# Banded attention scores: two triangles of a block pair folded into one 128-key square, and unfolded by GpSimd after the transposes

## The chip, the cores and the metric

The kernel runs on one core of a Trainium2 chip. The metric is the device time of one execution in microseconds; the median of a few runs is compared. A profile is one further execution, taken with the hardware profiler. The engines are named as in the profile: PE (TensorE), DVE (VectorE), ACT (ScalarE), POOL (GpSimd), SP (SyncE, which issues transfers).

## The reference

One decoder layer over 2048 tokens of width 1024. A normalised and modulated input `h` goes through one combined projection. Eight heads do forgetting attention over all earlier tokens. Eight query heads in two key/value groups do sliding-window attention with rotary positions and a learned sink; this is the part that the change touches:

```python
kk, vv = with_prev(k), with_prev(v)          # each block of 128 queries sees its own 128 keys and the 128 before
s = jnp.einsum('bnqhgd,bnshd->bnhgqs', qb, kk) * (d ** -0.5)
rel = i + Q_BLOCK - j                         # i: query in the block, j: key among the 256
band = (rel >= 0) & (rel < WINDOW)            # WINDOW = 128
s = jnp.where(mask, s, -jnp.inf)
p = jax.nn.softmax(jnp.concatenate([s, sink], axis=-1), axis=-1)[..., :-1]
out = jnp.einsum('bnhgqs,bnshd->bnqhgd', p, vv)
```

Query i sees, of its own block, the keys 0 to i, and, of the block before, the keys i+1 to 127: two complementary triangles, always 128 keys in all. The first block has no block before it. Each branch's output is gated, both go through one output projection, and the result is normalised and added to the input.

## The kernel before

The program is one sequence of stages: modulation and transposes of the input (to about 148 us), the banded heads together with projections (to about 440 us), the forgetting heads with the remaining projections, and the output projection. Most matrix products are in split f16: each operand is a high and a low half, and three products (high by high, high by low, low by high) replace an f32 one.

The banded heads are done in 32 windows (`Pair(j, i)`: head pair j, query blocks i and i+1; so two heads by two blocks). The order of the work is written out by hand: each engine's queue holds its instructions in the order in which the program records them. The stage's loop does this for window n:

```python
tick()
if n: wd.maxima()
fill(part[0]); tick()
if n: wd.exps()
fill(part[1]); tick(); fill(part[2]); tick(); fill(part[3])
if n: windows[n - 1].pv()
wd.turn()
if n + 1 < NW: windows[n + 1].scores()
```

`fill` puts projection units on PE (three matmuls of 512 columns, line 332, or twelve of 128, line 350) and runs the events that go with them: weight loads, their maximum (`w_max`), its way to DRAM and back to all partitions (`mx_d`, `mxr`, issued by POOL), and the split of weights into halves. `after(k, f)` runs f at the k-th following `tick`, which is how evacuations of PSUM follow the matmuls.

The steps of a window:

- `scores` (line 870): PE writes up to 256 scores for each of 128 queries, two heads and two blocks, into two PSUM banks (`pss`).
- `maxima` (line 883): one fused DVE instruction for each head and block adds the band mask `bmask`, scales, writes the result to `sm_` in SBUF and accumulates the maximum, starting from the sink. POOL copies the sink's value into a 257th column (line 881). `nb` is the negated maximum (line 887).
- `exps` (line 894): ACT takes the exponential of 257 columns, four times, with row sums.
- `turn` (line 903): PE transposes each block of 128 keys in f32, eight for a window, six where the first block of the sequence is in it, into `pxb` (two PSUM banks). At the next tick ACT copies the high half to f16 (line 912), and at the one after that DVE subtracts it for the low half (line 908); both are in `ptb`.
- `pv` (line 922), at the end of the next window: 24 matmuls multiply the transposed probabilities with the values; DVE divides by the sums at the next tick (line 928).

The pools of `pss`, `sm_`, `pxb` and `ptb` have one buffer each. POOL's queue in this stage holds also the stores of the gates (`z_d`, line 374) and of the outputs (`o_d`), and the weight loads.

Of the kernel before, what the change touches and what calls it, by code (L numbers as in the profile page):

```python
# [10 lines left out]
F32 = mybir.dt.float32  # L11
F16 = mybir.dt.float16
BF16 = mybir.dt.bfloat16
I32 = mybir.dt.int32
AF = mybir.ActivationFunctionType
ALU = mybir.AluOpType
AX = mybir.AxisListType

P = 128
# [7 lines left out]
EPS = 1e-6  # L27
PS_SCALE = 2.0 ** -25
NEG = -1.0e30
VB = P + 8  # L30
LIFT = 10.0 * math.log(2.0)
LIFT_A = 3.0 * math.log(2.0)
# [9 lines left out]
def hybrid_layer(  # L42
# [17 lines left out]
    V, A, G, PE, SP = nc.vector, nc.scalar, nc.gpsimd, nc.tensor, nc.sync  # L60
# [12 lines left out]
    const = ctx.enter_context(tc.tile_pool(name="const", bufs=1))  # L73
# [7 lines left out]
    def sm(n, tag):  # L81
        return small.tile([P, n], F32, tag=tag, name=tag)
# [79 lines left out]
    bmask = const.tile([P, 2 * P], F32, name="bmask")  # L162
# [33 lines left out]
    def after(n, f):  # L196
        late.append([n, f])
# [86 lines left out]
        after(lag + 1, low)  # L284

    pws = {}
    scl, isc, czs, kaps = {}, {}, {}, {}

    def col(name):
        return const.tile([P, 1], F32, name=name)  # L290

    def w_done(key):

        kind, j = key[:2], key[2:]
        pw = pws[key]
        if kind == "qk":
            kap = kappa(pw, key)
            scl[key] = col(f"scl_{key}")
            V.tensor_scalar(scl[key][:], kap[:], kap[:], 0.125, op0=ALU.mult, op1=ALU.mult)
            isc[key] = col(f"isc_{key}")  # L300
            V.reciprocal(isc[key][:], scl[key][:])
        elif kind == "qb":
            kap = kappa(pw, key)
            scl[key] = col(f"scl_{key}")
            V.tensor_scalar(scl[key][:], kap[:], kaps["kb"][:], 0.125, op0=ALU.mult, op1=ALU.mult)
        elif kind == "va":
            kaps[key] = kappa(pw, key)
        else:
            czs[key] = col(f"cz_{key}")
            V.tensor_scalar(czs[key][:], pw[:], pH[:], 2.0 ** -29, op0=ALU.mult, op1=ALU.mult)  # L310
            n = int(j) + (4 if kind == "zb" else 0)
            V.tensor_tensor(fac8[:, n:n + 1], kaps["vb" if kind == "zb" else f"va{j}"][:], czs[key][:], op=ALU.mult)
# [131 lines left out]
    st = start.enter_context(tc.tile_pool(name="start", bufs=1, reuse_waits="tile"))  # L444
    wad = start.enter_context(tc.tile_pool(name="wad", bufs=8, reuse_waits="tile"))
    with tc.manual_schedule():
# [68 lines left out]
                V.tensor_reduce(dst[:, 4 * n:4 * n + 4], dg, axis=AX.X, op=ALU.add)  # L515


        zero = st.tile([P, 2 * P], F32, name="zero")
        V.memset(zero[:], 0.0)
        bm1 = st.tile([P, 2 * P], F32, name="bm1")  # L520

        G.affine_select(bm1[:], zero[:], [[-1, 2 * P]], ALU.is_ge, NEG, base=P, channel_multiplier=1)
        G.affine_select(bmask[:], bm1[:], [[1, 2 * P]], ALU.is_ge, NEG, base=-1, channel_multiplier=-1)
        dm32 = st.tile([P, P], F32, name="dm32")

        G.affine_select(dm32[:], zero[:, :P], [[-1, P]], ALU.is_ge, NEG, base=0, channel_multiplier=1)
        dm32t = st.tile([P, P], F32, name="dm32t")

        G.affine_select(dm32t[:], zero[:, :P], [[1, P]], ALU.is_ge, NEG, base=0, channel_multiplier=-1)

        G.affine_select(triu[:], ones[:], [[1, P]], ALU.is_ge, 0.0, base=0, channel_multiplier=-1)

# [13 lines left out]
        for _ in range(3):  # L546
            e = math.floor(math.log2(rest))
# [304 lines left out]
    class Pair:  # L852


        def __init__(self, j, i):
            self.j, self.i, self.g = j, i, j // 2

            self.blocks = [(i + e, max(i + e - 1, 0), 1 + min(i + e, 1)) for e in range(2)]
            self.at = [0, 2 * self.blocks[0][2]]
            self.nt = 2 * sum(b[2] for b in self.blocks)  # L860

        def scores(self):
            self.pss = ps_s.tile([P, 2, CH], F32, tag="s", name="pss")
            q = ab[self.j, self.i // 4]
            for e, (i, k0, nk) in enumerate(self.blocks):
                qo, o = (i % 4) * P, e * 2 * P
                for n, (a, b) in enumerate(((0, 0), (0, 1), (1, 0))):
                    for h in range(2):
                        r = slice(64 * h, 64 * h + 64)
                        PE.matmul(self.pss[:, h, o:o + nk * P], q[r, a, qo:qo + P],  # L870
                                  kst[self.g][r, b, k0 * P:(i + 1) * P], start=(n == 0), stop=(n == 2))

        def maxima(self):
            key = f"qb{self.j}"
            snk2 = snk[:, 2 * self.j:2 * self.j + 2]

            self.sm_ = sws.tile([P, 2, 2, 2 * P + 1], F32, tag="ss", name="sm_")
            m = sm(4, "b_m")
            for e, (i, k0, nk) in enumerate(self.blocks):
                w = nk * P  # L880
                G.tensor_copy(self.sm_[:, e, :, w:w + 1], snk2.unsqueeze(2))
                for h in range(2):
                    V.tensor_tensor_reduce(self.sm_[:, e, h, :w], self.pss[:, h, e * 2 * P:e * 2 * P + w],
                                           bmask[:, 2 * P - w:], scale=scl[key][:], scalar=snk2[:, h:h + 1],
                                           op0=ALU.add, op1=ALU.max, accum_out=m[:, 2 * e + h:2 * e + h + 1])
            self.nb = sm(4, "b_nb")
            V.tensor_scalar(self.nb[:], m[:], -1.0, LIFT, op0=ALU.mult, op1=ALU.add)

        def exps(self):
            self.rs = sm(4, "b_rs")  # L890
            for e, (i, k0, nk) in enumerate(self.blocks):
                for h in range(2):
                    p, c = self.sm_[:, e, h, :nk * P + 1], slice(2 * e + h, 2 * e + h + 1)
                    A.activation(p, p, AF.Exp, bias=self.nb[:, c], accum_out=self.rs[:, c])

        def turn(self):

            nt = self.nt
            px = ps_t.tile([P, 8, P], F32, tag="t", name="pxb")
            for e, (i, k0, nk) in enumerate(self.blocks):  # L900
                for h in range(2):
                    for b in range(nk):
                        PE.transpose(px[:, self.at[e] + h * nk + b, :], self.sm_[:, e, h, b * P:(b + 1) * P], ident[:])  # L903
            self.ptt = ptp.tile([P, 2, 8, P], F16, tag="pt", name="ptb")
            hi, lo = self.ptt[:, 0, 0:nt, :], self.ptt[:, 1, 0:nt, :]

            def low():
                V.tensor_tensor(lo, px[:, 0:nt, :], hi, op=ALU.subtract)
                self.rinv = sm(4, "b_ri")
                V.reciprocal(self.rinv[:], self.rs[:])  # L910

            after(1, lambda: A.activation(hi, px[:, 0:nt, :], AF.Copy))
            after(2, low)

        def pv(self):
            j, i = self.j, self.i
            po = ps_pv.tile([P, 4, 64], F32, tag="pv", name="pob")
            for e, (i_, k0, nk) in enumerate(self.blocks):
                for h in range(2):
                    for b in range(nk):  # L920
                        for n, (pp_, vv) in enumerate(((0, 0), (0, 1), (1, 0))):
                            PE.matmul(po[:, 2 * e + h, :], self.ptt[:, pp_, self.at[e] + h * nk + b, :],  # L922
                                      vb[:, k0 + b, self.g, 64 * vv:64 * vv + 64],
                                      start=(b == 0 and n == 0), stop=(b == nk - 1 and n == 2))
# [35 lines left out]
    for kind, j in (("zb", 0), ("zb", 1), ("va", 0), ("zb", 2), ("zb", 3), ("va", 1), ("va", 2)):  # L960
        key = f"{kind}{j}"
# [137 lines left out]
    with swa_order:  # L1099
        fill(N_PRO - 4, tick2)  # L1100
        psx.close()
        sws = swa_pool("sws", 1)
        ptp = swa_pool("ptp", 1)
        ps_s = swa_pool("ps_s", 1, space=PSUM)
        ps_t = swa_pool("ps_t", 1, space=PSUM)
# [4 lines left out]
        base = N_PRO  # L1110
# [616 lines left out]
```

## Time and profile before

| | |
|---|---|
| median of 3 runs | 1185.31 us (1185.02 to 1186.49) |
| the profiled execution | 1185.43 us, its span 1183.7 us |
| mean granted TensorE clock | 0.991 |
| PE busy | 1139.2 us (96%) |
| DVE busy | 941.4 us (80%) |
| ACT busy | 680.5 us (57%) |
| POOL busy | 115.8 us (10%) |

The span runs from the first to the last instruction; the execution's own time is 1.7 us longer. A row of the timeline gives start, duration, engine, line, operation, out<-in, shapes and a count of merged instructions; in brackets, how long the engine sat idle before it and what ended that. A row of a grouped view gives count, busy time, mean nanoseconds of one, and the idle time before. A row of the tile view gives shortest, median and longest duration in nanoseconds, first and last start, and the forms. A row of the waits gives who waited for whom, the sum in us, how often, and the longest. Matmul ends are modelled, and starts are the more exact.

### The profile page before, as it was taken

The numbers are of one execution on the slowest core, as the hardware profiler recorded it, in microseconds if no ns is written. First come the engines' busy times: TensorE is split into PE (matmuls) and PEld (weight loads), VectorE is DVE, ScalarE is ACT, GpSimd is POOL, SyncE is SP. The second block draws the span as 40 slices with busy tenths as digits, with TensorE's granted clock in tenths as the row PEclk, the third lists the DMA queues.
The fourth block names the chain that finished last, engine by engine and source line by source line (L and its number), as shares of the span: only waits on it lengthen the run. The fifth ranks groups of instructions, "written<-read, shape, count | busy, mean of one in ns | idle before, by whom it ended". The sixth has DMA issues, their size and how long they took to land.

```text
span 1183.7 us, 27198 instructions
## 1 busy us (share of the span) xinstructions
PE 1139.2 (96%) x10757; PEld 684.4 (58%) x10757; DVE 941.4 (80%) x2311; ACT 680.5 (57%) x1150; POOL 115.8 (10%) x231
## 2 busy tenths in 40 slices
PE   6899999999999999999999999999999999999997
PEld 2466555865557995555555555555555555544444
DVE  7876678687875766788998989888898797778885
ACT  2784445565654541376766766676676788643332
POOL 2000111213122111101000100001000000000000
PEclk9899999999999999999999999999999999999999
DMA  9745433324324414333325334223311227587743
GB/s 331 264 134 90 80 92 71 88 52 110 92 62 84 63 23 100 48 82 95 64 73 57 77 70 84 60 40 77 42 42 46 57 80 244 130 212 199 198 142 107
DMA packets 123484, 120.22 MB, mean 102 GB/s; under 512 B 64948, under 2 KB 100828, under 8 KB 123356
## 3 DMA queue, kind: packets, MB, share of 16 engines
q1 hardware_dynamic: 112088, 85.69, 26.8%
q0 software_dynamic: 10832, 32.50, 14.1%
q8 instruction: 84, 1.38, 0.6%
q14 instruction: 44, 0.36, 0.1%
q10 hardware_dynamic: 436, 0.28, 0.1%
HBM read 64.75 MB, written 25.18 MB: 76 GB/s over the span
## 4 chain that ended last, share of the span: by engine, by line
PE 78%; DVE 11%; DMA 5%; issue 2%; ACT 2%; SPq 1%; another core or an unknown queue 0%; DVEq 0%; ACTq 0%
PE bk L332 29%; PE bk L1520 13%; PE bk L350 7%; PE sta L1309 4%; PE bk L1259 4%; PE sta L1308 4%; PE poa L1334 3%; PE poa L1335 3%; PE poa L1332 3%; DMA wa<-in_w_ada_dram 2%; PE pxb L903 2%; PE pss L870 2%; PE pob L922 2%; DVE a_m L1262 2%; DMA qs<-qf 1%
## 5 line engine op out<-in xcount | busy, mean ns | idle before, releaser
L1315 ACT ACTIVATE p<-sta,lift,scl_qk 128x1024 f32<-128x1024 f32 (+2 forms) x160 | 171.8, 1074 | 130.9 <-PE sta L1309 81.8
L332 PE MATMUL bk<-hT,wh_qk 128*128 128x512 f16 x768 | 194.7, 378 | 0.0
L1322 DVE TENSOR_TENSOR pha<-p,pha 128x1024 f16<-128x1024 f32 (+2 forms) x160 | 169.0, 1056 | 0.2 <-ACT pha L1319 0.2
L1262 DVE TENSOR_REDUCE a_m<-bk 128x1 f32<-128x512 f32 x192 | 130.3, 685 | 46.2 <-PE bk L1259 45.2
L1520 PE MATMUL bk<-wohl,oz 128*128 128x512 f16 x744 | 165.3, 379 | 1.0 <-DVE oz L1469 0.7
L1319 ACT ACTIVATE pha<-p 128x1024 f16<-128x1024 f32 (+2 forms) x160 | 148.1, 926 | 5.9 <-PE poa L1335 1.2
L1520 PEld LDWEIGHTS <-oz 128*128 128x128 f16 x744 | 71.9, 99 | 82.7 <-DVE oz L1469 1.8
L1332 PE MATMUL poa<-vt,pha 128*128 128x65 f16 x1088 | 116.6, 193 | 0.8 <-DVE ona L1341 0.7
L1335 PE MATMUL poa<-vt,pha 128*128 128x65 f16 x1088 | 116.1, 192 | 1.4 <-DVE pha L1322 1.4
L1334 PE MATMUL poa<-vt,pha 128*128 128x64 f16 x1088 | 116.6, 194 | 0.0
L332 PEld LDWEIGHTS <-wh_qk 128*128 128x128 f16 x768 | 72.2, 97 | 74.3 <-issue 1.9
L1308 PE MATMUL sta<-T 128*128 128x512 f16 (+1 forms) x320 | 110.9, 347 | 2.8 <-ACT p L1315 2.7
L1259 PE MATMUL bk<-T 66*128 66x512 f16 (+2 forms) x320 | 109.7, 348 | 2.6 <-DVE a_m L1262 1.9
L1332 PEld LDWEIGHTS <-pha 128*128 128x128 f16 x1088 | 101.5, 96 | 15.5 <-DVE ona L1341 1.9
L1309 PE MATMUL sta<-T 69*128 69x512 f16 (+1 forms) x320 | 109.8, 348 | 0.0
L1334 PEld LDWEIGHTS <-pha 128*128 128x128 f16 x1088 | 100.9, 97 | 11.4
L1335 PEld LDWEIGHTS <-pha 128*128 128x128 f16 x1088 | 100.8, 99 | 1.8 <-DVE pha L1322 1.8
L332 PE MATMUL bk<-hT,wh_za 128*128 128x512 f16 x384 | 99.7, 378 | 0.0
L350 PE MATMUL bk<-wh_va,hT 128*128 128x128 f16 x1536 | 90.2, 219 | 3.7 <-issue 3.7
L350 PEld LDWEIGHTS <-hT 128*128 128x128 f16 x1536 | 87.1, 98 | 8.1 <-issue 6.1
L332 PE MATMUL bk<-hT,wh_zb 128*128 128x512 f16 x384 | 88.9, 379 | 0.0
L332 PE MATMUL bk<-hT,wh_qb 128*128 128x512 f16 x384 | 87.4, 379 | 0.0
(505 smaller groups left out, 1894.2 us busy)
## 6 DMA issues: line engine op xcount, KB each, us to landing
hT<-in_x_dram SPq DMA_DIRECT2D x20, 512.0 KB
wa<-in_w_ada_dram SPq DMA_DIRECT2D x16, 512.0 KB
z_d<-tz POOLq DMA_DIRECT2D x32, 256.0 KB, 3.0
T<-stq SPq DMA_DIRECT2D x64, 128.0 KB
T<-z_d SPq DMA_DIRECT2D x16, 512.0 KB
out_dram<-hT SPq DMA_DIRECT2D x15, 512.0 KB
xt<-in_x_dram SPq DMA_DIRECT2D x12, 512.0 KB
qs<-qf SPq DMA_DIRECT2D x80, 64.0 KB
```

The costliest lines, as they stand in the source:

```text
L332: PE.matmul(ps, whl[:, a, k, :], hT[ci][:, b, k, :], start=(k == 0 and n == 0), stop=(k == KT - 1 and n == 2))
L350: PE.matmul(ps[:, u * P:(u + 1) * P], hT[ci][:, a, k, u * P:(u + 1) * P], whl[:, b, k, :], start=(k == 0 and n == 0), stop=(k == KT - 1 an ...
L1259: PE.matmul(mx[:, :w], T[0:XM, 0, i * P:(i + 1) * P], T[0:XM, 2, pc * CH:pc * CH + w], start=True, stop=True)
L1262: V.tensor_reduce(m3[:, u, pc:pc + 1], mx[:, :w], axis=AX.X, op=ALU.max)
L1308: PE.matmul(self.st[:, o:o + w], T[:, 3, kb_], T[:, 1, qc], start=True, stop=False)
L1309: PE.matmul(self.st[:, o:o + w], T[0:XR, 2, kb_], T[0:XR, 0, qc], start=False, stop=not diag)
L1315: A.activation(self.p32[:, :self.w], self.st[:, :self.w], AF.Exp, scale=scl[f"qk{self.hd}"][:], bias=lift[:])
L1322: V.tensor_tensor(self.ph[:, 1, :self.w], self.p32[:, :self.w], self.ph[:, 0, :self.w], op=ALU.subtract)
L1332: PE.matmul(po[:, u, :], ph[:, 0, pq], vt[:, b, hd, 0:65], start=(self.first and n == 0 and u == 0), stop=False)
L1334: PE.matmul(po[:, u, 0:64], ph[:, 0, pq], vt[:, b, hd, 65:VW], start=False, stop=False)
L1335: PE.matmul(po[:, u, :], ph[:, 1, pq], vt[:, b, hd, 0:65], start=False, stop=(self.last and n == len(self.blocks) - 1))
L1520: PE.matmul(py, self.hl[:, i, k, :], w_slot(8 * j + k)[:, cc], start=(k == 0 and m_ == 0), stop=(k == KT - 1 and m_ == 2))
```

## The change

The two triangles of a query block are put into one square of 128 keys before the maximum is taken, so that one block is transposed for each head and query block instead of two, and the two triangles are separated again after the transposition.

- `scores` writes the same products; where there is only one key block it goes to the second half.
- `maxima` works in PSUM. A predicated copy puts, wherever the own block's key lies after the query, the score of the block before in its place (the mask `dmask` read as 16-bit integers). A small copy puts the sink, divided by the score scale (`snd`, made in `w_done`), in the column before the square. One DVE reduction takes the maximum of 4 x 129 columns, and `nb` is scaled by `nscl`. In the four windows with the first block, DVE first fills the missing block with `LOWEST`.
- `exps` reads PSUM, with the scale in the instruction, 129 columns, and writes `sm_`.
- `turn` transposes four blocks. ACT's high half and DVE's low half go to a new tile `fold`. Four POOL selects then write `ptb`: for the high and the low half, one keeps the triangle of the block before and fills zeros, the other that of the own block.
- `pv` has the same matmuls on the new layout. `bmask` and its two selects are gone.

```diff
@@ w_done, for "qb" @@
+            nscl[key] = col(f"nscl_{key}")
+            V.tensor_scalar(nscl[key][:], scl[key][:], -1.0, None, op0=ALU.mult)
+            snd[key] = const.tile([P, 2], F32, name=f"snd_{key}")
+            isc_ = sm(1, "w_sw")
+            V.reciprocal(isc_[:], scl[key][:])
+            V.tensor_scalar(snd[key][:], snk[:, 2 * int(j):2 * int(j) + 2], isc_[:], None, op0=ALU.mult)
@@ scores @@
-                qo, o = (i % 4) * P, e * 2 * P
+                qo, o = (i % 4) * P, e * 2 * P + (2 - nk) * P
@@ maxima @@
-            self.sm_ = sws.tile([P, 2, 2, 2 * P + 1], F32, tag="ss", name="sm_")
+            s4 = self.pss[:].rearrange("p h (e c) -> p e h c", e=2)
+            if self.i == 0:
+                V.memset(s4[:, 0, :, 0:P], LOWEST)
+            V.copy_predicated(s4[:, :, :, P:2 * P], dmask[:].bitcast(I16).unsqueeze(1).unsqueeze(1).broadcast_to([P, 2, 2, P]),
+                              s4[:, :, :, 0:P])
+            V.tensor_copy(s4[:, :, :, P - 1:P], snd[key][:].unsqueeze(1).unsqueeze(3).broadcast_to([P, 2, 2, 1]))
+            self.s4 = s4[:, :, :, P - 1:2 * P]
             m = sm(4, "b_m")
-            for e, (i, k0, nk) in enumerate(self.blocks):
-                w = nk * P
-                G.tensor_copy(self.sm_[:, e, :, w:w + 1], snk2.unsqueeze(2))
-                for h in range(2):
-                    V.tensor_tensor_reduce(self.sm_[:, e, h, :w], self.pss[:, h, e * 2 * P:e * 2 * P + w],
-                                           bmask[:, 2 * P - w:], scale=scl[key][:], scalar=snk2[:, h:h + 1],
-                                           op0=ALU.add, op1=ALU.max, accum_out=m[:, 2 * e + h:2 * e + h + 1])
+            V.tensor_reduce(m[:].rearrange("p (e h) -> p e h", e=2), self.s4, axis=AX.X, op=ALU.max)
             self.nb = sm(4, "b_nb")
-            V.tensor_scalar(self.nb[:], m[:], -1.0, LIFT, op0=ALU.mult, op1=ALU.add)
+            V.tensor_scalar(self.nb[:], m[:], nscl[key][:], LIFT, op0=ALU.mult, op1=ALU.add)
@@ exps @@
-            for e, (i, k0, nk) in enumerate(self.blocks):
-                for h in range(2):
-                    p, c = self.sm_[:, e, h, :nk * P + 1], slice(2 * e + h, 2 * e + h + 1)
-                    A.activation(p, p, AF.Exp, bias=self.nb[:, c], accum_out=self.rs[:, c])
+            self.sm_ = sws.tile([P, 4, P + 1], F32, tag="ss", name="sm_")
+            for n in range(4):
+                A.activation(self.sm_[:, n], self.s4[:, n // 2, n % 2], AF.Exp, scale=scl[key][:],
+                             bias=self.nb[:, n:n + 1], accum_out=self.rs[:, n:n + 1])
@@ turn @@
-                        PE.transpose(px[:, self.at[e] + h * nk + b, :], self.sm_[:, e, h, b * P:(b + 1) * P], ident[:])
-            self.ptt = ptp.tile([P, 2, 8, P], F16, tag="pt", name="ptb")
-            hi, lo = self.ptt[:, 0, 0:nt, :], self.ptt[:, 1, 0:nt, :]
+            for n in range(4):
+                PE.transpose(px[:, n, :], self.sm_[:, n, 1:P + 1], ident[:])
+            self.ptt = ptp.tile([P, 2, 2, 4, P], F16, tag="pt", name="ptb")
+            fold = ptp.tile([P, 2, 4, P], F16, tag="fo", name="fold")
             def low():
-                V.tensor_tensor(lo, px[:, 0:nt, :], hi, op=ALU.subtract)
+                V.tensor_tensor(fold[:, 1], px[:], fold[:, 0], op=ALU.subtract)
                 self.rinv = sm(4, "b_ri")
                 V.reciprocal(self.rinv[:], self.rs[:])
-            after(1, lambda: A.activation(hi, px[:, 0:nt, :], AF.Copy))
+                for n in range(2):
+                    G.affine_select(self.ptt[:, 0, n], fold[:, n], [[0, 4], [-1, P]], ALU.is_ge, 0.0,
+                                    base=-1, channel_multiplier=1)
+                    G.affine_select(self.ptt[:, 1, n], fold[:, n], [[0, 4], [1, P]], ALU.is_ge, 0.0,
+                                    base=0, channel_multiplier=-1)
+            after(1, lambda: A.activation(fold[:, 0], px[:], AF.Copy))
             after(2, low)
@@ pv @@
-                            PE.matmul(po[:, 2 * e + h, :], self.ptt[:, pp_, self.at[e] + h * nk + b, :],
+                            PE.matmul(po[:, 2 * e + h, :], self.ptt[:, b + 2 - nk, pp_, 2 * e + h, :],
```

More of the change, by code (lines that the diff above doesn't have):

```diff
@@ L13 @@
 BF16 = mybir.dt.bfloat16
+I16 = mybir.dt.int16
 I32 = mybir.dt.int32
@@ L29 @@
 NEG = -1.0e30
+LOWEST = -3.0e38
 VB = P + 8
@@ L515, in ada_col @@
                 V.tensor_reduce(dst[:, 4 * n:4 * n + 4], dg, axis=AX.X, op=ALU.add)
-        zero = st.tile([P, 2 * P], F32, name="zero")
+        zero = st.tile([P, P], F32, name="zero")
         V.memset(zero[:], 0.0)
-        bm1 = st.tile([P, 2 * P], F32, name="bm1")
-        G.affine_select(bm1[:], zero[:], [[-1, 2 * P]], ALU.is_ge, NEG, base=P, channel_multiplier=1)
-        G.affine_select(bmask[:], bm1[:], [[1, 2 * P]], ALU.is_ge, NEG, base=-1, channel_multiplier=-1)
         dm32 = st.tile([P, P], F32, name="dm32")
-        G.affine_select(dm32[:], zero[:, :P], [[-1, P]], ALU.is_ge, NEG, base=0, channel_multiplier=1)
+        G.affine_select(dm32[:], zero[:], [[-1, P]], ALU.is_ge, NEG, base=0, channel_multiplier=1)
         dm32t = st.tile([P, P], F32, name="dm32t")
-        G.affine_select(dm32t[:], zero[:, :P], [[1, P]], ALU.is_ge, NEG, base=0, channel_multiplier=-1)
+        G.affine_select(dm32t[:], zero[:], [[1, P]], ALU.is_ge, NEG, base=0, channel_multiplier=-1)
         G.affine_select(triu[:], ones[:], [[1, P]], ALU.is_ge, 0.0, base=0, channel_multiplier=-1)
@@ L858, in __init__ @@
             self.blocks = [(i + e, max(i + e - 1, 0), 1 + min(i + e, 1)) for e in range(2)]
-            self.at = [0, 2 * self.blocks[0][2]]
-            self.nt = 2 * sum(b[2] for b in self.blocks)
         def scores(self):
@@ L896, in turn @@
+            for n in range(4):
+                A.activation(self.sm_[:, n], self.s4[:, n // 2, n % 2], AF.Exp, scale=scl[key][:],
+                             bias=self.nb[:, n:n + 1], accum_out=self.rs[:, n:n + 1])
         def turn(self):
[L898 to L903, printed above, removed]
@@ L904, in turn @@
[L904 to L905 removed]
+            px = ps_t.tile([P, 4, P], F32, tag="t", name="pxb")
+            for n in range(4):
+                PE.transpose(px[:, n, :], self.sm_[:, n, 1:P + 1], ident[:])
+            self.ptt = ptp.tile([P, 2, 2, 4, P], F16, tag="pt", name="ptb")
+            fold = ptp.tile([P, 2, 4, P], F16, tag="fo", name="fold")
             def low():
[L908 removed]
+                V.tensor_tensor(fold[:, 1], px[:], fold[:, 0], op=ALU.subtract)
```

5 lines of the change are left out of this document (2 added, 3 removed).

## The prediction

> **What bounds the kernel now.** The page first, for the whole run; then the busy time by stretches across the stage that the diff touches (the banded windows, from about 148 to 440 us).
>
> ```profile
> span 1183.7 us, 27198 instructions
> PE 1139.2 (96%) x10757; PEld 684.4 (58%) x10757; DVE 941.4 (80%) x2311; ACT 680.5 (57%) x1150; POOL 115.8 (10%) x231
> PE 78%; DVE 11%; DMA 5%; issue 2%; ACT 2%; SPq 1%; another core or an unknown queue 0%; DVEq 0%; ACTq 0%
> 230.00:270.00 40.00, 40.00 (x435) 26.54 (x432) 31.22 (x92) 24.05 (x67) 6.92 (x16) 1.00 0.24 58
> 350.00:390.00 40.00, 37.35 (x515) 29.98 (x514) 26.76 (x76) 20.45 (x60) 8.34 (x18) 0.96 0.38 78
> ```
>
> The stretch rows give PE, PEld, DVE, ACT and POOL busy time, the granted clock and the DMA share. PE is busy for 40.00 of 40 us: in this stage a microsecond of PE work removed is a microsecond gained, as long as nobody makes PE wait. DVE has a quarter of each stretch free, ACT 40%, POOL 80%. PE is 96% busy over the whole run, so what is gained here is carried to the end.
>
> **PE: the turns.** One window is one `Pair`. Its turns and the scores of the next follow each other:
>
> ```profile
> L908 DVE TENSOR_TENSOR ptb<-pxb,ptb x32: 947/1216/1219, 162.1 to 431.5; 128x1024 f16<-128x1024 f32 x28, 128x768 f16<-128x768 f32 x4
> L912 ACT ACTIVATE ptb<-pxb x32: 810/1023/1023, 158.5 to 429.0; 128x1024 f16<-128x1024 f32 x28, 128x768 f16<-128x768 f32 x4
> 227.03 0.85 PE L903 MATMUL pxb<-ident,sm__2890 128*128 128x128 f32 x6
> 227.81 0.83 PE L870 MATMUL pss<-kst,stb 64*128 64x256 f16 x12
> 260.79 1.07 PE L903 MATMUL pxb<-ident,sm__3510 128*128 128x128 f32 x8
> 261.79 0.83 PE L870 MATMUL pss<-kst,stb 64*128 64x256 f16 x12
> ```
>
> 28 windows turn eight blocks and four turn six, 248 in all; afterwards 32 turn four, 128. So 120 turns go. Eight take 1.00 us to the next scores and six take 0.78, or 0.11 us for one: 120 x 0.11 = 13.2 us of PE. Scores and products keep their counts.
>
> **DVE and ACT.** Timeline of one window, the nearest rows for the new operations, and two small operations:
>
> ```profile
> 262.80 0.54 DVE L883 CUSTOM_DVE_ANT_0 sm__3627<-pss,bmask,snk 128x256 f32<-128x256 f32 x1 [1.26 <-PE pss L870]
> 264.78 0.17 DVE L887 TENSOR_SCALAR b_nb<-b_m 128x4 f32<-128x4 f32 x1
> 264.86 0.68 DVE L372 SCALAR_TENSOR_TENSOR tz<-tz,bk 128x512 f32<-128x512 f32 x1
> 265.05 0.51 ACT L894 ACTIVATE sm__3627<-sm__3627,b_nb 128x257 f32<-128x257 f32 x1 [1.83 <-DVE b_nb L887]
> 265.46 1.22 DVE L908 TENSOR_TENSOR ptb<-pxb,ptb 128x1024 f16<-128x1024 f32 x1
> 265.84 0.55 POOL L374 DMA_DIRECT2D z_d<-tz  x1 [3.52 <-DVE tz L372]
> 268.39 0.86 PE L922 MATMUL pob<-vb,ptb 128*128 128x64 f16 x24
> L1264 DVE CUSTOM_DVE_ANT_0 bk<-bk,cmask 128x512 f32<-128x512 f32 x32 | 22.3, 697 | 2.1 <-PE bk L1259 2.1
> L1264 DVE CUSTOM_DVE_ANT_0 bk<-bk,cmask 128x256 f32<-128x256 f32 x32 | 13.8, 431 | 1.7 <-PE bk L1259 1.6
> L1262 DVE TENSOR_REDUCE a_m<-bk 128x1 f32<-128x512 f32 x192 | 130.3, 685 | 46.2 <-PE bk L1259 45.2
> 28.59 0.15 DVE L604 COPY mxs<-bk 128x2 f32<-128x2 f32 x1
> 28.77 0.15 DVE L87 TENSOR_SCALAR w_p<-mxs 128x1 f32<-128x1 f32 x1
> 151.61 0.40 ACT L894 ACTIVATE sm__1811<-sm__1811,b_nb 128x129 f32<-128x129 f32 x1 [3.14 <-DVE b_nb L887]
> ```
>
> Maxima before: from 262.80 to 264.95, 2.15 us. Afterwards four operations, each needing the one before: the predicated copy, 512 elements a row, PSUM to PSUM with an operand in SBUF. No row shows it; L1264 has the same places and length, 0.70 us, and I take that. Its bounds are 0.43 (two elements for one, as L1264 at 256) and 1.39 (two passes). Then the sink column 0.15, the maximum over 4 x 129 0.69 (L1262), the bias 0.17, and 0.03 between each two (28.59+0.15 to 28.77): 1.80. That is 0.35 sooner (0.6 sooner to 0.35 later by the bounds).
>
> The subtraction: L908 falls by 0.27 us from 1024 to 768 columns, hence 0.68 at 512, 0.54 sooner. ACT's copy L912 falls by 0.21 for 256, hence 0.60 instead of 1.02. The exponentials go from 0.51 to 0.40 each. They now read PSUM, which frees the scores' banks later; but the next scores stand behind the turns, and these wait for the exponentials anyway. DVE loses 0.9 us and ACT 0.8 us a window. Neither is the bound: no gain. Four LOWEST fills, the twelve small operations of `w_done`, and two mask selects fewer at the start come out at nothing, under DVE's free quarter.
>
> **POOL: the selects, and the wait they add.** Selects of the same instruction in the trace, back to back:
>
> ```profile
> 6.94 0.40 POOL L523 TENSOR_SCALAR_AFFINE_SELECT bmask<-bm 128x256 f32<-128x256 f32 x1
> 7.29 0.30 POOL L526 TENSOR_SCALAR_AFFINE_SELECT dm<-zero 128x128 f32<-128x128 f32 x1
> 7.53 0.30 POOL L529 TENSOR_SCALAR_AFFINE_SELECT dm32t<-zero 128x128 f32<-128x128 f32 x1
> ```
>
> From one start to the next it takes 0.35 us at 256 columns and 0.24 at 128, 0.11 per 128, which makes 0.57 at 512; the duration goes from 0.30 to 0.40, which makes 0.60. No row has 512 columns or f16, so this is an extension of the row. Four make 2.3 us a window, 73 us over 32 windows, on an engine 80% free. In the built program the first two selects wait for ACT's high half only (L912). It ends 2.8 us before L908 starts in the first window (158.5 + 0.81 to 162.1) and 1.5 us before it in the last (429.0 + 1.02 to 431.5), so the two, 1.17 us, are done when the subtraction ends. Only the second two follow it: 0.57 + 0.60 = 1.17 us, plus the hand-over from DVE to POOL (264.86 + 0.68 to 265.84: 0.3), between L908 and the products L922. Queued behind these on PE are the turns, the next scores and all projections.
>
> How much room is there? L908's end against the first L922, in 31 windows; the first, two of the tightest with what stood before one of them, and the last:
>
> ```profile
> 162.08 0.95 DVE L908 TENSOR_TENSOR ptb<-pxb,ptb 128x768 f16<-128x768 f32 x1
> 165.04 0.69 PE L922 MATMUL pob<-vb,ptb 128*128 128x64 f16 x18
> 184.68 0.83 PE L870 MATMUL pss<-kst,stb 64*128 64x256 f16 x12
> 187.49 0.54 DVE L883 CUSTOM_DVE_ANT_0 sm__2270<-pss,bmask,snk 128x256 f32<-128x256 f32 x1 [2.87 <-remote]
> 190.98 1.22 DVE L908 TENSOR_TENSOR ptb<-pxb,ptb 128x1024 f16<-128x1024 f32 x1
> 191.28 0.22 PE L922 MATMUL pob<-vb,ptb 128*128 128x64 f16 x2
> 241.50 1.22 DVE L908 TENSOR_TENSOR ptb<-pxb,ptb 128x1024 f16<-128x1024 f32 x1
> 242.77 0.86 PE L922 MATMUL pob<-vb,ptb 128*128 128x64 f16 x24
> 422.77 1.22 DVE L908 TENSOR_TENSOR ptb<-pxb,ptb 128x1024 f16<-128x1024 f32 x1
> 427.20 0.86 PE L922 MATMUL pob<-vb,ptb 128*128 128x64 f16 x24
> ```
>
> From 2.0 us (the first) to 3.2 (the last), with a median of 2.2. Three windows are late already (-0.9 at 190.98; -0.4; -0.1), three have 0.05, 0.5 and 0.6, and the next are 1.1, 1.1, 1.4, 1.6 and up. Counted from the end of the scores, PE comes to its products as before, and they are ready at -0.35 -0.54 +0.3 +1.17 = 0.6 us later. Were that all, the six tight windows would lose 0.6+0.6+0.6+0.55+0.1+0 = 2.5 us. But in the three late ones, and in the one with 0.5, DVE began the maxima (L883) 2 us or more after the scores ended (185.51 to 187.49 here), because of older work; and 0.9 us of DVE work goes from each window, more than the 0.6. There the wait shrinks. Between 2.5 lost and 0.4 gained, I take 1.0 lost.
>
> A page of the Trainium skill speaks against this placing: "GPSIMD Engine Reference", section "Elementwise — side-by-side cycle accounting", measures 769 ns for 512 elements in a tight loop of the GpSimd cores, against the 0.57 extended from this trace. By it two selects end 0.4 us later, the tight windows lose 1.4 to 4.9 us, and the time would be about 1175.
>
> **The sum.** The profiled execution took 1185.43 us (its span is 1183.7), and the median of the runs is 1185.31, 0.1 below. 1185.4 - 13.2 + 1.0 = 1173.2.
>
> **Rivals.**
> 1. *Costlier selects, slower.* The trace shows only f32 selects with one row of elements; these write f16 with four. If one costs s, the products are ready at -0.59 + 2s after before. Summed over the 31 rooms, a shift of 1.0 us costs 1.4 to 4.9 us, 1.6 costs 6 to 10, 2.0 costs 10 to 15, 3.0 some 31 to 36. So 1.1 us a select still leaves about 1180; the gain is gone near s = 1.35, 2.4 times the row; at s = 1.8 it is 1185.4 - 13.2 + 33, near 1205. For it: nothing but the missing row. Against: the regular slope. Chances: doubled, 0.12; slower, 0.12.
> 2. *Transfers behind the selects.* POOL also issues the weights' maxima and their way back.
>
> ```profile
> DVE w_mx L240 <- DMA mxr<-mx_d: 3.0, 2, 1.9
> L743 DVE TENSOR_TENSOR qs<-qs,sinT 128x512 f32<-128x512 f32 x15 | 10.3, 684 | 0.1
> 379.93 0.27 PE L350 MATMUL bk<-wh_va,hT 128*128 128x128 f16 x2 [2.65 <-issue]
> ```
>
> DVE waits for them twice already, 1.9 us at most, ahead of maxima. A window's selects can hold that queue for 2.3 us; of this the room left over, 2.2 - 0.6 = 1.6, covers all but 0.7 us a key. With the two keys that wait now that is 1.4 us, with all ten of the stage 7: 1175 to 1180. Against it: in the built queue a key's second transfer mostly stands behind selects that are over by then. Chance 0.08. A long stand-still of PE would also cost clock: the stretch from 350 us, with the 2.65 us quoted here, was granted 0.96, which is 1.6 us of 40; selects that cost under 1 us a window do not come near it.
> 3. *DVE and POOL in each other's way.* If operations like L743, with two inputs in SBUF, exclude a select, the 15 of L743 and the like of L744 and L737 (31 us) meet POOL's 73 us in 285 one time in four; 45 waits of some 0.3 us at 26% are 3.5 us, on the path only in tight windows: 1174 to 1177, chance 0.08. The Trainium skill has that rule ("SBUF — State Buffer", section "Who interferes with whom": an exclusive lock for the whole instruction); no row of before shows the two together.
> 4. *It doesn't do what it says.* If PE's freed time were filled by another wait, PE would show idle time before L332 or L350 and the run would stay within 0.2% of 1185.4. The next engine, DVE, would be at (31 - 4.8 x 0.9) / 37.9 = 71%. Chance 0.05.
>
> **How the numbers follow.** The forecast has 0.55, rivals 2 and 3 0.16, doubled selects 0.12: these are faster, 0.83, less 0.03 for their tails near no change: 0.80. Same has 0.03 + 0.05 = 0.08, slower 0.12. A change under 0.2% (2.4 us) can't be told from none here. The range starts at 1168.6: all 13.2 us kept, the window at 190.98 mended (0.9), and PE's stand-still before 379.93 (2.65, of which the profile shows no cause) gone. It ends at 1181.0, the doubled select; that leaves out rivals 4 and the slower end of 1, 0.17.
>
> **What would show it.** Right: turns x4 with 0.56 us to the scores, PE still 40 of 40 us in the stretches between 230 and 350, selects near 0.6 us, and few PE waits that POOL ends, under 1 us each. Wrong: "PE pob <- POOL" among the longest waits, selects over 1.2 us, a predicated copy over 1.4, or L240 waiting more than 3 us in sum.

## The result: 7.6 us faster, of 12.2 forecast

| kernel | median of runs | range | ratio to before, 95% interval |
|---|---|---|---|
| before | 1185.16 us | 1183.95 to 1186.49 (4 runs) | |
| changed | 1177.54 us | 1176.95 to 1179.14 (4 runs) | 0.9938 (0.992 to 0.9955) |

The profiled execution of the changed kernel took 1176.95 us, its span 1175.2. The sign was right and the time lies in the range (1168.6 to 1181.0), 4.3 us above the forecast. The page first (span, busy times, chain), then the stretches of the stage (PE, PEld, DVE, ACT, POOL busy, granted clock, DMA share, GB/s):

```profile
span 1175.2 us, 26821 instructions
PE 1127.3 (96%) x10637; PEld 671.1 (57%) x10637; DVE 935.1 (80%) x2167; ACT 662.0 (56%) x1150; POOL 192.6 (16%) x293
PE 71%; DVE 11%; issue 8%; DMA 5%; ACT 2%; POOL 2%; SPq 0%; DVEq 0%; ACTq 0%; POOLq 0%
```

```profile
230.00:270.00 40.00, 38.54 (x397) 23.65 (x395) 31.79 (x70) 20.38 (x63) 17.12 (x26) 1.00 0.24 54
270.00:310.00 40.00, 36.88 (x291) 19.15 (x288) 31.82 (x68) 20.88 (x66) 21.55 (x33) 1.00 0.39 99
310.00:350.00 40.00, 39.73 (x326) 21.63 (x327) 29.10 (x62) 19.64 (x65) 18.55 (x29) 0.96 0.30 81
350.00:390.00 40.00, 39.42 (x603) 32.27 (x602) 29.34 (x67) 20.94 (x63) 20.09 (x30) 1.00 0.39 82
```

POOL stands on the chain with 2%, where before it was not named, and PE is no longer busy 40 of 40 us: 1.5 us are missing between 230 and 270 and 3.1 between 270 and 310. Behind the longest of these waits, near 309 us, the clock falls too: 0.80 and 0.77 were granted in the 4 us from 308 and from 312, and 0.96 in the stretch from 310, which had 1.00 before; that is 1.6 us of its 40. DVE was to lose 0.9 us a window, which is over 4 us of a stretch; it has 31.79 where before it had 31.22. Where that went is seen in the groups of instructions (count, busy time, mean nanoseconds of one, idle time before; the last row is from the kernel before, for the stage alone):

```profile
L909 POOL TENSOR_SCALAR_AFFINE_SELECT ptb<-fold 128x512 f16<-128x512 f16 x64 | 46.5, 726 | 86.0 <-DVE fold L905 56.0 <-ACT fold L914 29.9
L911 POOL TENSOR_SCALAR_AFFINE_SELECT ptb<-fold 128x512 f16<-128x512 f16 x64 | 44.9, 701 | 0.0
L884 DVE TENSOR_REDUCE b_m<-pss 128x4 f32<-128x516 f32 x32 | 22.2, 695 | 1.1
L879 DVE COPY_PREDICATED pss<-dmask,pss 128x512 f32<-128x512 int16 x32 | 22.2, 694 | 18.0 <-PE pss L871 17.0 <-ACT fold L914 0.9
L905 DVE TENSOR_TENSOR fold<-pxb,fold 128x512 f16<-128x512 f32 x32 | 21.9, 683 | 0.0
L746 DVE TENSOR_TENSOR qs<-qs,sinT 128x512 f32<-128x512 f32 x20 | 19.7, 987 | 11.9 <-DMA cosT<-cs__234 7.9 <-DMA qs<-qf 3.7
L914 ACT ACTIVATE fold<-pxb 128x512 f16<-128x512 f32 x32 | 19.0, 594 | 35.7 <-issue 25.4 <-PE pxb L900 10.3
L280 DVE TENSOR_TENSOR oh<-on,oh 128x256 f16<-128x256 f32 x24 | 14.0, 582 | 0.0
L279 DVE TENSOR_TENSOR oh<-on,oh 128x256 f16<-128x256 f32 x23 | 9.2, 401 | 0.0
```

The new operations have the sizes of the forecast: the predicated copy 0.69 us (0.70 taken), the maximum 0.70, the subtraction 0.68, ACT's copy 0.59. What is out of place are two lines that the change doesn't touch: L746, the rotary product that was L743 before, went from 0.69 to 0.99 us in the mean, and L280, the low half of the output (L279 before), which took 0.40, takes 0.58. Both read two operands from SBUF. L905, with one operand in PSUM, stays at 0.68. The tile view shows that L746 has a median of 0.69 us and a longest of 3.20; the timeline shows one of the long ones:

```profile
279.17 0.55 POOL L381 DMA_DIRECT2D z_d<-tz  x1 [2.84 <-DVE tz L379]
279.48 3.19 DVE L746 TENSOR_TENSOR qs<-qs,sinT 128x512 f32<-128x512 f32 x1
279.72 0.65 POOL L909 TENSOR_SCALAR_AFFINE_SELECT ptb<-fold 128x512 f16<-128x512 f16 x1
280.31 0.64 POOL L911 TENSOR_SCALAR_AFFINE_SELECT ptb<-fold 128x512 f16<-128x512 f16 x1
280.90 0.63 POOL L909 TENSOR_SCALAR_AFFINE_SELECT ptb<-fold 128x512 f16<-128x512 f16 x1
281.48 0.63 POOL L911 TENSOR_SCALAR_AFFINE_SELECT ptb<-fold 128x512 f16<-128x512 f16 x1
282.70 0.69 DVE L747 TENSOR_TENSOR qc<-qc,qs 128x512 f32<-128x512 f32 x1
```

All four selects run while DVE stands in one product: it ends at 282.67, 0.56 us after the last of them (282.11), so it can have had little of its 0.69 us before. In this window the first two selects were not done early, as the forecast had it, since GpSimd's queue held the gates' store L381 ahead of them, and that waited 2.84 us for DVE. (In 28 of the 32 windows they were done before the subtraction ended; in four, all four selects ran back to back.) Undisturbed selects are 0.59 us apart (280.31 to 280.90). The most expensive place is the window near 309 us:

```profile
307.28 0.68 DVE L905 TENSOR_TENSOR fold<-pxb,fold 128x512 f16<-128x512 f32 x1
307.97 0.71 DVE L262 SCALAR_TENSOR_TENSOR wh_qb<-wr_qb,w_sw,wh_qb 128x512 f16<-128x512 f32 x1
308.03 1.15 POOL L909 TENSOR_SCALAR_AFFINE_SELECT ptb<-fold 128x512 f16<-128x512 f16 x1 [0.69 <-DVE fold L905]
308.61 1.12 DVE L740 TENSOR_TENSOR stb<-qc,stb 128x512 f16<-128x512 f32 x1
309.14 1.08 POOL L911 TENSOR_SCALAR_AFFINE_SELECT ptb<-fold 128x512 f16<-128x512 f16 x1
309.24 0.26 PE L924 MATMUL pob<-vb,ptb 128*128 128x64 f16 x3 [2.19 <-POOL ptb L909]
310.27 1.09 PE L924 MATMUL pob<-vb,ptb 128*128 128x64 f16 x19 [0.78 <-POOL ptb L911]
```

Here the subtraction is late, each of the two selects behind it takes 1.1 us instead of 0.6, the first beside DVE's L262, the second beside L740 (a product that takes 0.68 us undisturbed and 1.12 here), and PE stands still for 2.19 + 0.78 us. The waits of the whole run (who for whom: sum, times, longest):

```profile
PE pob L924 <- POOL ptb L909: 3.5, 3, 2.2
PE pob L924 <- POOL ptb L911: 3.1, 7, 0.8
DVE w_mx L241 <- DMA mxr<-mx_d: 3.4, 2, 3.1
```

PE waits 6.6 us for selects. Three theories stood against each other: **A**, the selects only stand in the path, as forecast; **B**, selects and DVE's products with two operands in SBUF exclude each other; **C**, the weights' maxima (L241) land later than the shorter windows allow, and DVE is late through them.

### The profile page after: what moved, and what is told of

Same layout as the page of the kernel before. It is cut to its first block, busy times and chain, and to the rows that moved or that the text cites. A ratio compares the mean times of both kernels' runs of the same rounds, so it can differ in the third digit from the quotient of the medians.

```text
span 1175.2 us, 26821 instructions
## 1 busy us (share of the span) xinstructions
PE 1127.3 (96%) x10637; PEld 671.1 (57%) x10637; DVE 935.1 (80%) x2167; ACT 662.0 (56%) x1150; POOL 192.6 (16%) x293
## 4 chain that ended last, share of the span: by engine, by line
PE 71%; DVE 11%; issue 8%; DMA 5%; ACT 2%; POOL 2%; SPq 0%; DVEq 0%; ACTq 0%; POOLq 0%
PE bk L339 24%; PE bk L1522 13%; PE bk L357 7%; PE sta L1311 4%; PE sta L1310 4%; PE bk L1261 4%; PE poa L1336 3%; PE poa L1337 3%; PE poa L1334 3%; DMA wa<-in_w_ada_dram 2%; PE pob L924 2%; PE pss L871 1%; DVE a_m L1264 1%; DVE pha L1324 1%; PE pxb L900 1%
## 5 line engine op out<-in xcount | busy, mean ns | idle before, releaser
L357 PE MATMUL bk<-wh_va,hT 128*128 128x128 f16 x1536 | 89.9, 219 | 0.0
L357 PEld LDWEIGHTS <-hT 128*128 128x128 f16 x1536 | 87.1, 98 | 4.1 <-issue 2.1
```

The lines of the kernel that those rows point to most:

```text
L357: PE.matmul(ps[:, u * P:(u + 1) * P], hT[ci][:, a, k, u * P:(u + 1) * P], whl[:, b, k, :], start=(k == 0 and n == 0), stop=(k == KT - 1 an ...
```

## The experiments

All were timed beside the kernel before, which had medians of 1185.2, 1186.1 and 1185.6 us on the chips of the three groups. The changed kernel itself was not timed again with them, so a difference from its 1177.54 us holds to about 1 us (an estimate from these three medians).

**No selects.** The four selects are left out, and `pv` reads `self.fold[:, pp_, 2 * e + h, :]`.

> The changed kernel without its four selects a window: the products read the folded square itself (both triangles, so the output is not the reference's). PE, DVE and ACT keep all their instructions. The changed kernel takes 1177.5 us; its trace shows 6.7 us in which PE waits for a select ahead of the products. Theory A (the selects are late as forecast, about 1.0 us on the path and nothing more): 1176 to 1177. Theory B (the selects and DVE's operations with two inputs in SBUF exclude each other, which draws out both and makes the products late): all 6.7 us go and so does the stretch of halved clock behind the longest of them (about 1.6 us): 1168.5 to 1171; L746 is back from 0.99 to 0.69 us and L886 from 0.26 to 0.17. Theory C (what makes the maxima late is the landing of the weights' maxima, L241, which now comes in shorter windows): L241 still waits 3 us, window 18 still leaves PE idle for 1 to 2 us with the halved clock behind it: 1171.5 to 1174.

Measured: 1174.09 us (1171.45 to 1176.24). L746 is at 0.69 us again, DVE is busy for 919.4 us in all instead of 935.1, and no select ends a wait. That is 3.4 us less than the changed kernel, so A is too small. But 1168.5 was not reached: the profiled run has PE standing still for something else.

```profile
PE bk L357 <- issue: 5.2, 2, 2.6
PE pxb L900 <- issue: 1.2, 1, 1.2
```

The kernel before had the same kind of stand-still (2.65 us ahead of L350); the changed kernel's profiled run had none so long. They differ from one kernel's profile to another's, and the runs of this kernel are 4.8 us apart. L886 stayed at 0.23 us: its new form costs that, not the selects.

**Earlier transfers.** In `add`, the leads of load, maximum and way back:

```diff
-(42, w_load), (31, w_max), (21, w_back)
+(46, w_load), (35, w_max), (25, w_back)
```

> The changed kernel with the weights' loads, their maxima and the way back each begun four units of projection earlier (46, 35 and 25 units ahead instead of 42, 31 and 21); the scale that waits for them stays at 12. Everything is computed. Theory C: L241's waits (3.4 us in two) fall under 1 us, window 18 loses its 2.97 us of PE idle and the halved clock behind it: 1172.5 to 1174.5. Theory B: L241's waits fall, but selects and DVE still meet, other windows keep their 0.2 to 0.9 us each and window 18 keeps about half: 1175.5 to 1178. Theory A: no change, 1177 to 1178.

Measured: 1185.73 us (1178.12 to 1190.97, 12 runs), 8 us slower than the changed kernel. In the list of waits L241 has one left, of 1.8 us, and the window near 309 didn't notice:

```profile
308.75 0.26 PE L924 MATMUL pob<-vb,ptb 128*128 128x64 f16 x3 [2.19 <-POOL ptb L909]
309.79 1.19 PE L924 MATMUL pob<-vb,ptb 128*128 128x64 f16 x19 [0.77 <-POOL ptb L911]
```

But the wait that is left is the one ahead of this window, and it is as long as in the changed kernel, where the profile names no releaser for it (the first row; the second is of this run):

```profile
293.72 0.29 DVE L241 TENSOR_REDUCE w_mx<-mxr 128x1 f32<-128x128 f32 x1 [1.89 <-issue]
293.25 0.28 DVE L241 TENSOR_REDUCE w_mx<-mxr 128x1 f32<-128x128 f32 x1 [1.85 <-DMA mxr<-mx_d]
```

What the edit took away are the waits at 171 and 423 us, so the run doesn't test C where it matters. The timelines of both runs speak for a part of C in this window: from L241 on DVE works without a pause to the next maxima, ACT's exponentials follow, behind them ACT's half of a weight split, for which DVE stands idle another 2.07 us, and from there DVE works without a pause to the late subtraction. In the changed kernel B may feed this too, since DVE takes the maximum that goes into this transfer at 283.64, behind the product of 3.19 us. The 8 us are a cost of the edit that none of the theories had. In its profiled run, part of it is one wait of PE for the first transposed keys behind the stage (DMA T<-stq), 4.3 us against 1.3 in the changed kernel, and a stand-still of 2.7 us ahead of L357.

**The same in the kernel before.**

> The kernel before with the same three leads moved by four units. It is the control for the run above: before has no selects in its windows, and PE is busy 40 of 40 us in two of the stretches where L240 waits. Theory C, if it holds for the changed kernel alone: 1184 to 1186, no change. If the earlier loads cost or bring something of their own (their buffers, other places of DVE's maxima), it shows here, by at most 1.5 us either way, and is taken off the result above. Theories A and B: 1184 to 1186 too.

Measured: 1184.50 us (1182.39 to 1187.75, 12 runs), ratio 0.9995 (0.9984 to 1.0006). The leads alone cost the kernel before nothing; why they cost the changed one 8 us stays open beyond the parts named.

**Memsets for selects.** Each select becomes `G.memset(fold[:, n], 0.0)`.

> The changed kernel with each select replaced by a GpSimd memset of the same half of the folded square, at the same place in the queue and behind the same waits; the products read the square (the output is not the reference's: the probabilities become zero). GpSimd then writes SBUF but reads nothing there. Theory B, with the exclusion lying in GpSimd's reads (as the Trainium skill, SBUF - State Buffer, section Who interferes with whom, has it: two SBUF inputs of DVE against an instruction of GpSimd that reads): L746 back to 0.69 us, DVE's two-input operations as short as before, products less late: 1169 to 1173. Theory B with any use of SBUF by GpSimd excluding DVE: L746 near 0.95 us and 1175 to 1178. Theory A (the queue and its hand-over cost, not the exclusion): the memsets hold the products as the selects did, 1176 to 1177.5, with L746 whichever.

Measured: 1176.01 us (1174.49 to 1176.75).

```profile
L746 DVE TENSOR_TENSOR qs<-qs,sinT 128x512 f32<-128x512 f32 x20 | 13.7, 687 | 11.0 <-DMA sinT<-sp__232 7.6 <-DMA qs<-qf 3.3
L910 POOL MEMSET fold<- 128x512 f16 x128 | 65.1, 523 | 116.8 <-DVE fold L904 113.1
```

L746 is back at 0.69 us and L280 at 0.40 though GpSimd is busy beside them: without GpSimd's reading nothing is drawn out. The rule of the Trainium skill that rival 3 named ("SBUF — State Buffer", section "Who interferes with whom") says just that, and the trace agrees: 0.69 beside writes, 0.99 beside selects. The time says less than hoped, since all four memsets overwrite what the subtraction reads and so stand behind it, 2.1 us in place of two selects' 1.2; PE waits some 5 us for them. So time in the queue costs without any exclusion too, and of the expectations the time meets that of theory A.

**Selects that nobody reads.** All selects run; `pv` reads the square as in the first run.

> The changed kernel with all its selects running as before, but with the products reading the folded square itself, so that nobody waits for a select (the output is not the reference's). The selects still read SBUF beside DVE. If what the selects cost is the products' wait: 1173 to 1175, as without selects, though L746 stays near 0.99 us. If DVE's drawn-out operations cost by themselves: 1176 to 1177.5.

Measured: 1172.63 us (1171.95 to 1175.37).

```profile
L746 DVE TENSOR_TENSOR qs<-qs,sinT 128x512 f32<-128x512 f32 x20 | 19.4, 972 | 10.9 <-DMA sinT<-sn__233 6.5 <-DMA qs<-qf 4.2
PE pob L925 <- DVE fold L905: 2.6, 2, 1.9
```

DVE's products are as drawn out as in the changed kernel, and 4.9 us are gone all the same. So most of what the selects cost is the wait of the products. The remaining 2.6 us are two windows in which the subtraction itself is late, 0.7 us near 183 and 1.9 near 305; ahead of the second, DVE had stood idle for L241 for 2.05 us. In the run without selects that idle time was 1.01 us and the products waited 0.2 us in all. So DVE's drawn-out work and theory C have a part in these two windows; the runs don't say which has how much.

**Each select twice.** `for n in (0, 0, 1, 1)`.

> The changed kernel with every select issued twice, four behind the subtraction instead of two (nothing else changes, the second writes the same). It tests the price list of the rooms: by the rooms of the kernel before, a select of 0.59 us twice makes the products 1.2 us later than now, 1.8 us later than before the change, which the list puts at 8 to 13 us lost against 1.0 for the forecast: 1180 to 1185. If the exclusion between selects and DVE grows with the selects' time (91 us now, 180 then), the products come later still and the windows lag: 1185 to 1195. If the selects were hardly on the path: 1177 to 1179.

Measured: 1211.99 us (1210.78 to 1213.34), above every expectation.

```profile
PE pob L924 <- POOL ptb L909: 22.0, 15, 3.8
PE pob L924 <- POOL ptb L911: 7.2, 20, 0.7
L746 DVE TENSOR_TENSOR qs<-qs,sinT 128x512 f32<-128x512 f32 x20 | 27.9, 1396 | 12.1 <-DMA sinT<-sn__233 6.4 <-DMA qs<-qf 5.6
```

L746 is at 1.40 us, and in 20 of the 32 windows PE waits. The list of rooms gave 1180 to 1185; it came out 34 us above the changed kernel. The list counted the selects at their undisturbed length and left the DVE behind them as it was; the granted clock is lower too, 0.982 to 0.986 in its runs against 0.989 to 0.992.

**Unfolding on DVE.** Two `tensor_tensor` multiplications of 1024 columns by a mask `tri`, no selects.

> The changed kernel with the unfolding on DVE: two multiplications of 1024 columns by masks of 0 and 1 behind the subtraction, in place of GpSimd's four selects. Everything is computed. No row of the changed kernel has such an operation; by the subtraction of 1024 columns before the change it is 1.22 us, 2.4 us a window, 78 us of DVE, which is busy 29 of 40 us now and would be at 41: DVE becomes the bound, 1185 to 1200. If f16 with both inputs in SBUF runs at twice that pace (0.65 us), DVE stands at 36 of 40 and the products come as with the selects: 1176 to 1181. No exclusion is left in either: L746 back at 0.69 us.

Measured: 1179.10 us (1174.65 to 1181.18).

```profile
L912 DVE TENSOR_TENSOR ptb<-fold,tri 128x1024 f16<-128x1024 f16 x64 | 41.4, 688 | 0.0
PE pob L926 <- DVE ptb L912: 3.9, 7, 1.6
```

0.69 us for 1024 columns, the faster case. The rotary product is back at 0.69 us, but 1.4 us of DVE a window stand in the path: no better than GpSimd.

**High selects early.** The two selects of the high half move from `low` into the step of ACT's copy, ahead of the transfers that GpSimd's queue gets between.

```diff
-            after(1, lambda: A.activation(fold[:, 0], px[:], AF.Copy))
+            after(1, high)      # ACT's copy, then the two selects of fold[:, 0]
```

> The changed kernel with the two selects of the high half issued right behind ACT's copy, one step of the order ahead of the subtraction and of what GpSimd issues between (the output's and the logs' transfers), so that at most two selects stand back to back more often than four. In the changed kernel two operations of L746 took 3.19 us and one of L280 2.93, each from before a chain of four selects to its end. Theory B, with the length of the chain as the price: no DVE operation over 2.2 us, L746's mean under 0.90 us (0.99 now), and of the 4.9 us between the changed kernel and the run whose selects nobody reads, one to three come back: 1174.5 to 1176.5. If the chain doesn't matter: L746 near 0.99, 1177 to 1178.5.

Measured: 1175.32 us (1174.96 to 1177.73), 2.2 less than the changed kernel; the intervals of the two ratios overlap (0.9903 to 0.9929 here, 0.992 to 0.9955 there). The tile view of L746 (shortest, median, longest):

```profile
L746 DVE TENSOR_TENSOR qs<-qs,sinT x20: 659/692/1172, 67.9 to 381.0; 128x512 f32<-128x512 f32 x20
```

The longest is 1.17 us instead of 3.20, the mean 0.76, and in no window do four selects run back to back. So the longest meetings had the length of the chain of selects, as expected. What that is worth in time stays open: near 309 us PE waits 1.7 us instead of 3.0, but there L241 had kept DVE idle for 1.16 us instead of 1.89.

**Products a quarter of a window later.**

```diff
             fill(part[0])
+            if n > 1: windows[n - 2].pv()
...
-            if n: windows[n - 1].pv()
             wd.turn()
```

Not shown: `ptb` is allocated in `low` instead of `turn`, and the products of the last window but one follow the loop.

> The changed kernel with the products of a window a quarter of a window later: instead of standing in front of the turns of the next window, they stand behind the first quarter of the projections of the window after it, so that their selects have some 3.5 us more (the turns, the scores and that quarter). No instruction is added or taken away; everything is computed. Without its selects the changed kernel took 1174.1 us, with them 1177.5. If the selects cost through the wait of the products alone (PE waits 6.7 us for them in the profiled run), it goes: 1172.5 to 1174.5, no row of PE that a select ends. If the 15 us by which DVE's two-input operations are drawn out make the exponentials and turns late, that stays: 1176 to 1177.5, and PE waits ahead of L900. If the later products collide with something of their own (the output's evacuation, the folded square's single buffer), 1176 to 1180.

Measured: 1169.68 us (1169.16 to 1170.17), ratio 0.9863 (0.9847 to 0.988): the best version that computes everything, 16.4 us under the kernel before and 7.9 under the changed one.

```profile
230.00:270.00 40.00, 40.00 (x406) 24.55 (x405) 32.72 (x74) 22.39 (x71) 19.69 (x30) 1.00 0.30 75
270.00:310.00 40.00, 39.05 (x327) 20.80 (x326) 33.17 (x75) 20.00 (x63) 19.15 (x31) 1.00 0.34 84
L746 DVE TENSOR_TENSOR qs<-qs,sinT 128x512 f32<-128x512 f32 x20 | 22.6, 1129 | 11.2 <-DMA sinT<-sn__233 7.8 <-DMA qs<-qf 3.1
```

PE is at 40.00 and 39.05 of 40 us. L746 is longer than in the changed kernel (1.13 us against 0.99), and it matters little: no wait of PE in the stage ends at a select, and 0.9 us of waits are left ahead of the turns.

**The same in the kernel before**, with two buffers for `ptb`.

> The kernel before with its products a quarter of a window later, at the place where they were put in the run of the changed kernel with late products (1169.7 us); the pool of ptb has two buffers for it. It is the control for that run. If the turns are worth the 13.2 us of the prediction and late products take every other difference away, the two differ by 13.2: 1182 to 1184. If the late products do nothing for the kernel before (PE waits 1.0 us for products in its profiled run): 1184.5 to 1186.5, and the change with late products is worth more than its turns.

Measured: 1184.87 us (1180.29 to 1188.38, 12 runs), ratio 0.9988 (0.9976 to 1.0). Late products do little for the kernel before. With them the change is worth 15.2 us by the medians (14.8 by the ratios, since the two ran on different chips), 2 more than its turns; with runs 8 us apart on one side, that difference stays open.

**Both.** Late products, early high selects, two buffers.

> The changed kernel with late products and with the high half's selects early, ptb in two buffers, so that no select waits for the products of the window before (55 us of GpSimd's idle time with late products alone). Everything is computed. PE stood still for 1.9 us in the stage with late products alone, of which 0.9 for exponentials that came late. If the drawn-out DVE operations made these late: 1168 to 1169.5. If nothing is left to gain: 1169 to 1170.5. A loss, over 1170.5, would come from selects that now fall on other DVE operations.

Measured: 1169.94 us (1166.41 to 1172.48), the same as late products alone. Nothing is left here that a select holds.

## Why the prediction was right, and where it was off

- **The turns, 13.2 us.** Right. Four turns to the next scores take 0.56 or 0.57 us in 29 of 31 windows (0.56 forecast):

```profile
299.57 0.63 PE L900 MATMUL pxb<-ident,sm__4104 128*128 128x128 f32 x4
300.14 0.83 PE L871 MATMUL pss<-kst,stb 64*128 64x256 f16 x12
```

  With everything in place but the wait for selects the kernel took 1172.6 us; the forecast without its last term was 1185.4 - 13.2 = 1172.2. That the two are 0.4 us apart is in part luck: PE still waits 2.6 us for products in that run, and late products came to 1169.7.
- **The maxima, 1.80 us.** 1.89, of which the predicated copy is 0.69. Not the bound, as said.
- **Select of 0.57 us, hand-over 0.3.** 0.59 undisturbed; the hand-over was shorter (subtraction's end 307.96, select 308.03). The 0.77 us per 512 elements of the Trainium skill's page ("GPSIMD Engine Reference", section "Elementwise — side-by-side cycle accounting") does not fit these selects; the estimate of about 1175 worked out from it lies nearer to the 1177.5, but what lengthened the selects was DVE, not their own pace.
- **The wait for the products, 1.0 us lost.** This is the term that was mis-sized: 4.9 us (against selects that nobody reads; 3.4 against none). Its working had three gaps. The rooms were taken with DVE as in the kernel before, less 0.9 us a window, so that the late windows were to mend themselves; the one near 191 us did, but three of DVE's products waited out whole chains of selects, and the other two (near 183 and 309 us) got worse. Two selects cost 1.17 us only alone; beside DVE's products they took up to 2.2. And the forecast left the clock out, as no window was to lose 1 us; the one near 309 lost 2.97, and the stretch behind it was granted 0.96.
- **Rival 3** was the main mechanism behind that, given 0.08 and 3.5 us of DVE, at 0.3 us a meeting. It came to 15.7 us of DVE (935.1 against 919.4 without selects). For the three lines that it counted the number of meetings was sound (13 operations drawn out, some 12 forecast), but they cost 8.9 us; L280 and the weight split L262, which it left out, add 4.3 and 1.5. Most meetings cost 0.1 to 0.5 us, near the price that it took. Three products, though, waited out a chain of four selects, 2.5 us each.
- **Rival 2** (transfers behind selects) can't be ruled out as a part. The longest idle time ahead of L241, 3.1 us, stands at 423 us, where no product waits; but the 1.9 us at 293 stand ahead of the window near 309. Over the runs, that idle time and PE's wait in that window were 1.9 and 3.0 us (changed kernel), 1.9 and 3.0 (earlier transfers), 2.1 and 1.9 (nobody reads), 1.2 and 1.7 (early high selects), 1.0 and none (no selects); in the kernel before, 1.9 and none. No run changes this transfer alone. The queue also mattered in a way that the rival did not have: a transfer that waits for DVE held the *selects* back and made the chain of four.
- **Rival 1's list** was far too cheap above one select: 1212 us, where it had 1180 to 1185 for twice the selects.
- **What would show it.** The selects' means (0.73 and 0.70) and the turns came as named, and so did two warnings: PE waiting 2.19 us for POOL, L241 over 3 us. The second came mostly from a place where no product waits. PE's 40 of 40 us between 230 and 350 did not come: 38.54, 36.88 and 39.73.

## What to carry to other kernels

Work that is moved to an idle engine is paid where it is waited for, so look at the room between producer and consumer first, and widen it in the same edit: here one call moved in the order was worth about as much (7.9 us) as the whole change before it (7.6 us), and in the kernel before, where the products had room, next to nothing. Before GpSimd is given operands in SBUF, look at what DVE does with two operands in SBUF at that time, and price a meeting at up to the whole run of GpSimd instructions back to back. Where GpSimd's queue also holds transfers that wait for DVE, put the early work ahead of them.

## What was not expected of the hardware

- A DVE product of 0.69 us stood for 3.19 us beside four selects in a row. Near 172 us product and select alternated instead, and a select took 1.15 us. In both cases the product's recorded start is the earlier one, by 0.24 and 0.07 us, so what decides between the two is not shown.
- A predicated copy of 512 columns, PSUM to PSUM with a mask in SBUF, takes 0.69 us; an f16 product of 1024 columns with both operands in SBUF takes the same 0.69.
- PE stood still for 1 to 2.7 us ahead of the projections L350 or L357 with no cause in the profile, in five of the thirteen kernels' profiles. It may be a part of why runs of one kernel differ by some us; no run shows that.
